# Padding tiles and a moved pool, so that the stage pools' tiles lie at multiples of 512 bytes

## The chip, the cores and the metric

The kernel runs on one core of a Trainium2 chip. TensorE multiplies, VectorE (DVE), ScalarE (ACT) and GpSimd (POOL) work on tiles, and SyncE (SP) issues nearly all DMAs. The metric is the time of the core in microseconds, as the median of several runs.

## The reference, cut to what matters

Two blocks run one after the other on 512 tokens of width 1024, in float32:

```python
# first block
h = rms_norm(x, ln_mix_g)
x = x + (sigmoid(m1) * (nsa_attention(h) @ w_branch_nsa) + sigmoid(m2) * (gla(h) @ w_branch_gla)) @ w_out
x = x + memory_cross_attention(rms_norm(x, ln_x_g), rms_norm(mem, ln_mem_g))   # @ w_xq, w_xkv, w_xo
x = x + ((gelu(conv3(u)) * g) @ w_down)        # u, g = split(rms_norm(x, ln_ffn_g) @ w_up), 2816 wide each
x = rms_norm(x, ln_final_g)
# second block
x = x + retention(rms_norm(x, ret_norm))       # 4 heads, w_in 1024x6144, w_out 2048x1024
x = x + ((silu(conv3(gate)) * val) @ w_down0)  # FFN, 2816 wide
x = x + stick_breaking(rms_norm(x, sb_norm))   # 16 heads of 64
x = x + ((silu(conv3(gate)) * val) @ w_down1)
return rms_norm(x, final_norm)
```

## The kernel before

**Products.** The activations are kept transposed, as 8 tiles xT of 128 x 512 floats. Every float32 operand of a large product is split into a rounded part (fp32r) and a rest, as hi and lo: `split` (L147) does it with one instruction of ScalarE (L148) and one of VectorE (L149). `mm3` (L171) then issues three products for each pair: both hi (L175), stationary hi with streamed lo (L176), stationary lo with streamed hi (L177). Each product loads a stationary operand of 128 columns (512 bytes in a partition) and streams a moving operand, mostly of 512 columns (2048 bytes). In the trace a product is written out<-moving,stationary.

**Weights.** `wload` (L159) brings a unit of 128 x 1024 floats by DMA into one of 2 buffers wr and splits it into one of 3 buffers wh and wl. A unit serves 24 products of 512 columns. In most projections (`fm_unit`, L179) the weight tile is stationary and the activation streams; in `tm_block` (L188) it is the other way round.

**Stages.** The program goes through the stages gla, nsa, mrg, xat (cross attention), ffa (first FFN), ret (retention), ffb, stk (stick-breaking) and ffc. Streamed by the large products are: xh and xl (the scaled input of each stage, split), mid (the hidden tiles of the FFNs, L854 and L149), yh and yl (outputs of retention heads), os (attention outputs), mix (the merged branches), ons (outputs of nsa), mm (the normalised memory, in mrg, both as moving and as stationary operand), wd (the weights of the last four outputs of ffc, as stationary operand, with 256 columns of mid), v and sT (values and scores of retention), pT (transposed weights of the nsa attention). The softmax of nsa reads a table, strip, that one DMA brings at the stage's start (L618).

**Places.** All tiles live in pools. The pools const, x, w and sm stand from low addresses up for the whole program; each `stage` opens two pools above them, first wk (all tiles of 2048 bytes) and then st, and closes them at its end; the pools mix and mem stand between sm and a stage's; the pool mixo (ons and share) stands at the other end. Tiles get addresses in the order of their pool. The pool sm holds small tiles and ends at 448 modulo 512. A tile's phase is its address in a partition modulo 512 bytes; the built programs have these:

| tiles | phase before | phase after |
|---|---|---|
| x, xh, xl (pool x); wr, wh, wl (pool w) | 0 | 0 |
| wk, mid, yh, yl, os, mix, mm, v, sT, kq, wd, khi, klo, qs, vhl, qh, ql, k, vh, hi, lo (stage pools, mix, mem) | 448 | 0 |
| ons, share (pool mixo) | 480 | 0 |
| pT of nsa | 288 | 0 |
| pr of nsa (transposed by TensorE) | 32 to 416 | 96 to 480 |
| pcmp and vcmp (pool sm) | 0 | 64 |
| rB, and acc of the sums of squares (pool sm) | 384, 0 | 448, 64 |
| sbtri_r, negones_r, negones (pool const, stationary in stk) | 448 | 448 |

The order of each engine's instructions is set by a scheduler when the program is built.

Of the kernel before, what the change touches and what calls it, by code (L numbers as in the profile page):

```python
# [10 lines left out]
F32 = mybir.dt.float32  # L11
F32R = mybir.dt.float32r
# [5 lines left out]
P = 128  # L18
# [47 lines left out]
def tile_blocks(ctx: ExitStack, tc: tile.TileContext, a: dict, out: bass.AP, dbg=None):  # L66
    nc = tc.nc
    act, dve, pool, pe, sync = nc.scalar, nc.vector, nc.gpsimd, nc.tensor, nc.sync

    cur = {}  # L70

    def sbpool(name, stack=ctx, side=None):
        kw = {} if side is None else {"side": side}
        return stack.enter_context(tc.tile_pool(name=name, bufs=1, reuse_waits="tile", **kw))
# [21 lines left out]
    def wkt(dt=F32):  # L96
        return cur["wk"].tile([P, S], dt, tag="wk", name="wk", bufs=cur["nwk"])

    def bank(tag="pa"):
        return cur["psum"].tile([P, S], F32, tag=tag, name=tag, bufs=cur["banks"][tag])  # L100
# [4 lines left out]
    def tiles(pool_, tag, n, bufs=None, dt=F32, w=S):  # L105
        return [pool_.tile([P, w], dt, tag=tag, name=tag, bufs=bufs or n) for _ in range(n)]
# [4 lines left out]
    sm_ = sbpool("sm")  # L111

    class sm:
        @staticmethod
        def tile(shape, dt, tag=None, name=None, bufs=4):
            return sm_.tile(shape, dt, tag=tag or name, name=name, bufs=bufs)


    g0 = cpool.tile([P, 2 * KD], F32, name="g0")
# [3 lines left out]
    def x_tile(k, dt=F32):  # L123
        return xpool.tile([P, S], dt, tag=f"x{k}", name=f"x{k}", bufs=1)
# [10 lines left out]
    def C(name, i=0, n=None):  # L135
        o, c = CST[name]
        return cst[:, o + i:o + i + (c if n is None else n)]
# [9 lines left out]
    def split(hi, lo, src):  # L147
        act.activation(hi, src, AF.Copy)  # L148
        dve.tensor_sub(lo, src, hi.bitcast(F32))  # L149
# [9 lines left out]
    def wload(src, own=None):  # L159
        n = src.shape[-1]  # L160
        raw = wpool.tile([P, UNIT], F32, tag="r", name="wr", bufs=NRAW)
        if own is None:
            hi = wpool.tile([P, UNIT], F32R, tag="h", name="wh", bufs=NSPL)
            lo = wpool.tile([P, UNIT], F32R, tag="l", name="wl", bufs=NSPL)
        else:
            hi, lo = own
        sync.dma_start(raw[:, :n], src)
        split(hi[:, :n], lo[:, :n], raw[:, :n])
        return hi, lo
# [143 lines left out]
    def mixer():  # L313
# [3 lines left out]
        with stage("gla", {"pp": 4, "pa": 3, "ss": 1}, 5) as st:  # L317
# [271 lines left out]
            for hd in range(4):  # L589
# [8 lines left out]
                hi, lo = x_tile(hd, F32R), x_tile(4 + hd, F32R)  # L598
# [7 lines left out]
        op = sbpool("mixo", hold, "right")  # L606
# [4 lines left out]
        def half_gate(m, j, dst):  # L611

            proj(16 + 8 * j + m, dst)
            act.activation(dst, dst, AF.Tanh, scale=0.5)

        with stage("nsa", {"pp": 2, "s": 3, "pt": 2, "po": 1}, 2) as st:
            strip = st.tile([P, NSTRIP], F32, name="strip")
            sync.dma_start(strip, a["strip"])  # L618

            pcmp = [sm.tile([P, S], F32R, tag="nrm", name="pcmp", bufs=3) for _ in range(2)]  # L620
            for x in pcmp:
                pool.memset(x.bitcast(F32), 0.0)

            def geometry(i):
                nk = P * (i + 1)
                w0 = P * max(0, i - 2)
                return nk, w0, nk - w0

            def softmaxes(kv, i):
                nk, w0, nw = geometry(i)  # L630
                nkp, nwp = max(256, nk), max(256, nw)
                ss = sm.tile([P, 4, 3], F32, tag="ss", name="ss")
                prs = []
                for g in range(4):
                    hd = 4 * kv + g
                    slope = 2.0 ** -(hd + 1)
                    qs = qh[hd][:, i * P:(i + 1) * P]
                    s0, s1 = bank("s"), bank("s")
                    for dst, (his, los), c in ((s0[:, :nkp], ks, slice(0, nkp)), (s1[:, :nwp], kw, slice(w0, w0 + nwp))):
                        pe.matmul(dst, qs, his[kv][:, c], start=True, stop=False)  # L640
                        pe.matmul(dst, qs, los[kv][:, c], start=False, stop=True)
                    for j in range(2):
                        pe.matmul(s1[:, 384:416], qs, kcmp[j][:, kv, :], start=j == 0, stop=j == 1)
                    pr = st.tile([P, NPR], F32, tag="pr", name="pr", bufs=5)
                    nm = sm.tile([P, 3], F32, tag="nm", name="nm")
                    c0 = 896 + 24 - 8 * i
                    segs = ((pr[:, 896:NPR], s1[:, 384:384 + NCMP], strip[:, c0:c0 + NCMP]),
                            (pr[:, 0:nk], s0[:, :nk], strip[:, 512 - nk:512]),
                            (pr[:, 512:512 + nw], s1[:, :nw], strip[:, 512 + 384 - nw:896]))
                    for b in (1, 2, 0):  # L650
                        dst, src, dist = segs[b]
                        dve.tensor_tensor_reduce(out=dst, in0=src, in1=dist, scale=slope, scalar=3e38, op0=OP.add,
                                                 op1=OP.min, accum_out=nm[:, b:b + 1])
                        act.activation(dst, dst, AF.Exp, scale=-1.0, bias=nm[:, b:b + 1],  # L654
                                       accum_out=ss[:, g, b:b + 1])
                    prs.append([x[0] for x in segs])
                dve.reciprocal(ss, ss)
                dve.tensor_mul(ss, ss, gates[:, i, 12 * kv:12 * kv + 12].rearrange("p (g b) -> p g b", g=4))
                if i == 0:
                    dve.tensor_mul(ss[:, :, 0], ss[:, :, 0], C("rowmask").to_broadcast([P, 4]))  # L660
                for g in range(4):
                    for b in (1, 2, 0):
                        scaler(b).tensor_scalar(prs[g][b], prs[g][b], ss[:, g, b:b + 1], 1.0, op0=OP.mult, op1=OP.mult)  # L663
                return prs

            def scaler(b):
                return pool if b == 1 else dve

            def values(kv, i, prs):
                nk, w0, nw = geometry(i)  # L670
                blocks = [(1, j * P, P, vhl[j][:, kv, :]) for j in range(i + 1)]
                blocks += [(2, j * P, P, vhl[w0 // P + j][:, 2 + kv, :]) for j in range(nw // P)]
                blocks += [(0, 0, NCMP, vcmp[:, kv, :])]
                po = bank("po")
                for x, (b, o, n, v) in enumerate(blocks):
                    pt = bank("pt")
                    for g in range(4):
                        pe.transpose(pt[0:n, g * P:(g + 1) * P], prs[g][b][:, o:o + n], ident)  # L678
                    hi, lo = tiles(st, "pT", 2, 4, F32R) if b else pcmp
                    split(hi[0:n], lo[0:n], pt[0:n])  # L680
                    for j, m in enumerate((hi, lo)):
                        pe.matmul(po, v, m, start=x + j == 0, stop=x == len(blocks) - 1 and j == 1)  # L682

                rows = slice(kv * 64, kv * 64 + 64)
                other = slice(64 - kv * 64, P - kv * 64)
                t = wkt()
                act.activation(t[rows], po[other], AF.Copy)
                dve.tensor_add(t[rows], t[rows], po[rows])
                src = t[rows].rearrange("p (g q) -> p g q", g=4)
                split(ons[0][rows, :, i * P:(i + 1) * P], ons[1][rows, :, i * P:(i + 1) * P], src)  # L690

            todo = [(kv, i) for kv in range(2) for i in (3, 2, 1, 0)]
            prev = None
            for kv, i in todo:
                prs = softmaxes(kv, i)
                if prev is not None:
                    values(*prev)
                prev = (kv, i, prs)
            values(*prev)
            ons_ = [(ons[0][:, g, :], ons[1][:, g, :]) for g in range(4)]  # L700


            share = tiles(op, "share", KD)
            for m2 in range(KD // 2):
                for m in (2 * m2, 2 * m2 + 1):
                    half_gate(m, 1, share[m])
                u = wload(a["w_branch_gla"][m2])
                for j in range(2):
                    m = 2 * m2 + j
                    pg = fm_unit(u, ogs, 4, off=j * 512)  # L710
                    dve.scalar_tensor_tensor(share[m], share[m], 1.0, pg, op0=OP.add, op1=OP.mult)
# [639 lines left out]
```

## Time and profile before

| | |
|---|---|
| median of 3 runs | 2341.67 us (2338.39 to 2344.12) |
| profiled execution | 2338.12 us, its span 2336.3 us |
| TensorE busy | 2294.6 us, 98% of the span, 10872 products |
| VectorE, ScalarE, GpSimd busy | 60%, 44%, 8% |
| mean granted clock of TensorE | 0.994 |

A product's record has a modelled end and is longer than the time to the next product's start; records overlap. Where TensorE has no idle time, the time goes by from start to start.

### The profile page before, as it was taken

How to read it: one execution, taken by the hardware profiler on the slowest of the kernel's cores; microseconds unless marked ns; L12 is line 12 of the kernel's file. 1: busy time of each engine (PE TensorE's matmuls, PEld its weight loads, DVE VectorE, ACT ScalarE, POOL GpSimd, SP SyncE). 2: the span in 40 equal slices, each digit the busy share in tenths (PEclk: the TensorE clock that was granted, in tenths of full speed). 3: DMA queues.
4: the chain of work that ended last, by engine and by line, in shares of the span. 5: the costliest groups of instructions: out<-in, count | busy, mean ns of one | idle time of the engine just before them, and what ended most of it. 6: DMA issues, size and time to landing. Idle time of an engine off the chain costs nothing.

```text
span 2336.3 us, 28002 instructions
## 1 busy us (share of the span) xinstructions
PE 2294.6 (98%) x10872; PEld 1881.3 (81%) x10872; DVE 1398.4 (60%) x2194; ACT 1021.6 (44%) x1662; POOL 194.0 (8%) x228
## 2 busy tenths in 40 slices
PE   8999999999999999999999999999999999999997
PEld 7787778878888888888887788888888887888886
DVE  5457875457545356545454674746577886747465
ACT  4345763444323234423323442424477884424243
POOL 2001110101000003000000100000121101000002
PEclk9999999999999999999999999999999999999998
DMA  4221032312222223222222232222344322222222
GB/s 159 91 64 54 28 118 98 115 66 100 99 91 99 95 90 113 82 91 81 81 90 73 81 108 90 99 92 93 98 118 105 91 64 81 99 98 92 99 92 71
DMA packets 66054, 213.41 MB, mean 91 GB/s; under 512 B 7793, under 2 KB 10114, under 8 KB 65794
## 3 DMA queue, kind: packets, MB, share of 16 engines
q1 hardware_dynamic: 60802, 203.24, 26.2%
q0 software_dynamic: 5120, 8.39, 1.7%
q8 instruction: 85, 1.39, 0.2%
q14 instruction: 47, 0.39, 0.1%
HBM read 201.11 MB, written 2.10 MB: 87 GB/s over the span
## 4 chain that ended last, share of the span: by engine, by line
PE 91%; DVE 4%; ACT 2%; issue 1%; POOL 1%; DMA 0%; SPq 0%; DVEq 0%; POOLq 0%; ACTq 0%
PE pp L176 26%; PE pp L175 26%; PE pp L177 26%; PE po L682 1%; DVE wl L149 1%; DVE xl L268 1%; PE pt L678 1%; ACT pr L654 1%; PE po L1143 1%; PE pp L1050 1%; PE pp L1052 1%; PE pp L1051 1%; POOL pr L663 1%; DVE x L298 1%; PE pa L982 1%
## 5 line engine op out<-in xcount | busy, mean ns | idle before, releaser
L148 ACT ACTIVATE wh<-wr 128x1024 fp32r<-128x1024 f32 (+2 forms) x368 | 384.3, 1044 | 790.4 <-PE pp L176 623.2
L175 PE MATMUL pp<-xh,wh 128*128 128x512 f32 x1612 | 634.9, 394 | 3.0 <-ACT xh L267 2.8
L176 PE MATMUL pp<-xl,wh 128*128 128x512 f32 x1612 | 631.8, 392 | 3.6 <-DVE xl L268 3.6
L177 PE MATMUL pp<-xh,wl 128*128 128x512 f32 x1612 | 632.0, 392 | 0.0
L149 DVE TENSOR_TENSOR wl<-wr,wh 128x1024 fp32r<-128x1024 f32 (+2 forms) x368 | 452.4, 1229 | 209.3 <-ACT wh L148 182.8
L175 PEld LDWEIGHTS pp<-xh,wh 128*128 128x128 f32 x1612 | 303.8, 189 | 66.8 <-ACT xh L267 4.1
L176 PEld LDWEIGHTS pp<-xl,wh 128*128 128x128 f32 x1612 | 303.9, 189 | 66.3 <-DVE xl L268 5.5
L177 PEld LDWEIGHTS pp<-xh,wl 128*128 128x128 f32 x1612 | 303.7, 188 | 62.7 <-issue 0.9
L298 DVE TENSOR_TENSOR x<-x,pp 128x512 f32<-128x512 f32 x130 | 89.2, 686 | 244.4 <-PE pp L177 244.3
L175 PE MATMUL pp<-mid,wh 128*128 128x512 f32 x504 | 198.9, 396 | 0.0
L176 PE MATMUL pp<-mid,wh 128*128 128x512 f32 x504 | 198.6, 395 | 0.0
L177 PE MATMUL pp<-mid,wl 128*128 128x512 f32 x504 | 198.5, 395 | 0.0
L237 POOL TENSOR_TENSOR acc<-acc 128x512 f32<-128x512 f32 (+1 forms) x60 | 80.4, 1340 | 913.0 <-ACT acc L233 839.1
L176 PE MATMUL pp<-wl,xh 128*128 128x512 f32 (+1 forms) x320 | 122.3, 382 | 4.0 <-DVE wl L149 4.0
L175 PE MATMUL pp<-wh,xh 128*128 128x512 f32 (+1 forms) x320 | 121.4, 381 | 0.8 <-ACT wh L148 0.8
L177 PE MATMUL pp<-wh,xl 128*128 128x512 f32 (+1 forms) x320 | 121.3, 380 | 0.0
L175 PEld LDWEIGHTS pp<-mid,wh 128*128 128x128 f32 x504 | 94.4, 187 | 24.8 <-ACT mid L148 2.0
L176 PEld LDWEIGHTS pp<-mid,wh 128*128 128x128 f32 x504 | 94.4, 187 | 23.7 <-DVE mid L149 0.9
L177 PEld LDWEIGHTS pp<-mid,wl 128*128 128x128 f32 x504 | 94.4, 187 | 22.8
L148 ACT ACTIVATE mid<-wk 128x512 fp32r<-128x512 f32 x66 | 41.5, 631 | 124.4 <-DVE wk L854 108.8
L827 ACT ACTIVATE wk<-wk,vec 128x512 f32<-128x512 f32 x110 | 88.6, 809 | 6.5 <-DVE wk L841 5.2
L829 DVE SCALAR_TENSOR_TENSOR wk<-wk,vec 128x510 f32<-128x510 f32 x110 | 82.3, 750 | 3.6
(426 smaller groups left out, 3369.3 us busy)
## 6 DMA issues: line engine op xcount, KB each, us to landing
wr<-in_up SPq DMA_DIRECT2D x88, 512.0 KB, 3.2
wr<-in_w_up SPq DMA_DIRECT2D x44, 512.0 KB, 3.2
wr<-in_w_in_fm SPq DMA_DIRECT2D x32, 512.0 KB, 3.6
wr<-in_ret_vg SPq DMA_DIRECT2D x32, 512.0 KB, 3.2
wr<-in_down SPq DMA_DIRECT2D x32, 512.0 KB, 3.2
wr<-in_w_down SPq DMA_DIRECT2D x16, 512.0 KB, 3.2
wr<-in_ret_qk SPq DMA_DIRECT2D x16, 512.0 KB, 3.3
wr<-in_ret_out SPq DMA_DIRECT2D x16, 512.0 KB, 3.3
```

The lines of the kernel that those rows point to most:

```text
L148: act.activation(hi, src, AF.Copy)
L149: dve.tensor_sub(lo, src, hi.bitcast(F32))
L175: pe.matmul(ps, sh, mh, start=first and i == 0, stop=False)
L176: pe.matmul(ps, sh, ml, start=False, stop=False)
L177: pe.matmul(ps, sl, mh, start=False, stop=last and i == n - 1)
L237: (dve if k == len(tiles) - 1 else pool).tensor_add(acc[:, :n], acc[:, :n], sq[:, :n])
L268: dve.scalar_tensor_tensor(lo, x, g, hi.bitcast(F32), op0=OP.mult, op1=OP.subtract)
L298: dve.tensor_add(xT[m], xT[m], ps)
L654: act.activation(dst, dst, AF.Exp, scale=-1.0, bias=nm[:, b:b + 1], accum_out=ss[:, g, b:b + 1])
L663: scaler(b).tensor_scalar(prs[g][b], prs[g][b], ss[:, g, b:b + 1], 1.0, op0=OP.mult, op1=OP.mult)
L827: act.activation(dst, src, AF.Identity, scale=V(wname, 2 * nw + j), bias=V(bname, j))
L829: dve.scalar_tensor_tensor(dst[:, 2:], src[:, :S - 2], V(wname, j), dst[:, 2:], op0=OP.mult, op1=OP.add)
```

## The change

A helper `fill` allocates a tile of n floats in a pool and sets it to zero. One of 16 floats (64 bytes) stands first in the pool sm, so that this pool, and all that stands above it, begins its tiles 64 bytes higher. One of 120 floats (480 bytes) stands last in mixo. The tiles pT of nsa go from the pool st, where they stood behind strip and pr, to the pool wk. The table above has the phases that follow.

```diff
@@ -114,6 +114,12 @@
         @staticmethod
         def tile(shape, dt, tag=None, name=None, bufs=4):
             return sm_.tile(shape, dt, tag=tag or name, name=name, bufs=bufs)
+
+    def fill(pool_, n):
+
+        pool.memset(pool_.tile([P, n], F32, name="fill"), 0.0)
+
+    fill(sm_, 16)
 
 
     g0 = cpool.tile([P, 2 * KD], F32, name="g0")
@@ -676,7 +682,7 @@
                     pt = bank("pt")
                     for g in range(4):
                         pe.transpose(pt[0:n, g * P:(g + 1) * P], prs[g][b][:, o:o + n], ident)
-                    hi, lo = tiles(st, "pT", 2, 4, F32R) if b else pcmp
+                    hi, lo = tiles(cur["wk"], "pT", 2, 4, F32R) if b else pcmp
                     split(hi[0:n], lo[0:n], pt[0:n])
                     for j, m in enumerate((hi, lo)):
                         pe.matmul(po, v, m, start=x + j == 0, stop=x == len(blocks) - 1 and j == 1)
@@ -701,6 +707,7 @@
 
 
             share = tiles(op, "share", KD)
+            fill(op, 120)
             for m2 in range(KD // 2):
                 for m in (2 * m2, 2 * m2 + 1):
                     half_gate(m, 1, share[m])
```

The instructions of TensorE, VectorE, ScalarE and SyncE stand in the same order in both programs; their lines are 6 or 7 higher after. GpSimd has two more, the memsets. Its rows at the start of the nsa stage, where it scales the softmax rows pr, with the semaphores that each waits for; before:

```order
L210 TENSOR_TENSOR y<-v,mhalf 128x16 [waits DVE_49]
L663 TENSOR_SCALAR pr<-pr,ss 128x512 [waits PE_49,DVE_49,Activation_49,Pool_49]
L663 TENSOR_SCALAR pr<-pr,ss 128x512 [waits Activation_49] x2
L663 TENSOR_SCALAR pr<-pr,ss 128x512 [waits DMAHW0_49,Activation_49]
L663 TENSOR_SCALAR pr<-pr,ss 128x384 [waits DVE_49,Activation_49]
```

and after:

```order
L216 TENSOR_TENSOR y<-v,mhalf 128x16 [waits DVE_49]
L120 MEMSET fill 128x120
L669 TENSOR_SCALAR pr<-pr,ss 128x512 [waits DVE_49,PE_49,Activation_49]
L669 TENSOR_SCALAR pr<-pr,ss 128x512 [waits PE_49,Activation_49,Pool_49]
L669 TENSOR_SCALAR pr<-pr,ss 128x512 [waits Activation_49] x2
L669 TENSOR_SCALAR pr<-pr,ss 128x384 [waits DVE_49,Activation_49]
```

The memset of 120 columns stands between two instructions of GpSimd and waits for nothing. On SyncE, at the same place of the program, the DMA of strip stands among loads of weights; before:

```order
L167 DMA wr<-in_w_in_fm 128x1024 [waits DMAHW7_49,DVE_49]
L167 DMA wr<-in_w_in_fm 128x1024 [waits DMAHW0_49,DVE_49]
L618 DMA strip<-in_strip 128x951 [waits DVE_49,PE_49,Pool_49]
L167 DMA wr<-in_w_branch_gla 128x1024 [waits DMAHW1_49,DVE_49]
L167 DMA wr<-in_w_in_fm 128x1024 [waits DMAHW2_49,DVE_49,Activation_49]
```

and after:

```order
L173 DMA wr<-in_w_in_fm 128x1024 [waits DMAHW7_49,DVE_49]
L173 DMA wr<-in_w_in_fm 128x1024 [waits DMAHW0_49,DVE_49]
L624 DMA strip<-in_strip 128x951 [waits Pool_49]
L173 DMA wr<-in_w_branch_gla 128x1024 [waits DMAHW1_49,DVE_49]
L173 DMA wr<-in_w_in_fm 128x1024 [waits DMAHW2_49,DVE_49,Activation_49]
```

Its place in the queue is the same, and it waits for one GpSimd instruction where it waited for VectorE, TensorE and GpSimd, since strip now lies over other tiles of the stage before.

## Rows read from the trace of the kernel before

**Rows 1.** Page, parts 1 and 4: TensorE's share; the chain by engine.

```profile
PE 2294.6 (98%) x10872; PEld 1881.3 (81%) x10872; DVE 1398.4 (60%) x2194; ACT 1021.6 (44%) x1662; POOL 194.0 (8%) x228
...
PE 91%; DVE 4%; ACT 2%; issue 1%; POOL 1%; DMA 0%; SPq 0%; DVEq 0%; POOLq 0%; ACTq 0%
```

**Rows 2.** Waits of TensorE, longest entry: us in total, times, longest.

```profile
PE pt L678 <- POOL pr L663: 4.0, 11, 0.7
```

**Rows 3.** TensorE by shape: count, busy us, mean ns, idle us before.

```profile
L175 PE MATMUL pp<-xh,wh 128*128 128x512 f32 x1612 | 634.9, 394 | 3.0 <-ACT xh L267 2.8 <-ACT wh L148 0.2
...
L175 PE MATMUL pp<-mid,wh 128*128 128x512 f32 x504 | 198.9, 396 | 0.0
...
L175 PE MATMUL pp<-wh,xh 128*128 128x512 f32 x288 | 112.4, 390 | 0.0
...
L175 PE MATMUL pp<-yh,wh 128*128 128x512 f32 x96 | 38.1, 397 | 0.0
...
L175 PE MATMUL pp<-os,wh 128*128 128x512 f32 x76 | 30.8, 406 | 0.3 <-DVE x L298 0.3
...
L175 PE MATMUL pp<-mix,wh 128*128 128x512 f32 x64 | 25.3, 395 | 0.0
...
L175 PE MATMUL pp<-ons,wh 128*128 128x512 f32 x32 | 12.7, 396 | 0.0
```

**Rows 4.** Two stretches of ffa by tile: ns min/median/max, first and last start.

```profile
L175 PE MATMUL pp<-mid,wh x64: 394/394/394, 625.5 to 669.6; 128*128 128x512 f32 x64
...
L175 PE MATMUL pp<-xh,wh x128: 388/389/395, 670.3 to 756.7; 128*128 128x512 f32 x128
```

**Rows 5.** Timeline, ends of stretches in ffa and ffc: start and duration, us.

```profile
625.50 0.39 PE L175 MATMUL pp<-mid,wh 128*128 128x512 f32 x1
...
670.06 0.39 PE L177 MATMUL pp<-mid,wl 128*128 128x512 f32 x1
670.29 0.39 PE L175 MATMUL pp<-xh,wh 128*128 128x512 f32 x1
...
757.13 0.39 PE L177 MATMUL pp<-xh,wl 128*128 128x512 f32 x1
...
2042.15 0.39 PE L175 MATMUL pp<-mid,wh 128*128 128x512 f32 x1
...
2086.90 0.39 PE L177 MATMUL pp<-mid,wl 128*128 128x512 f32 x1
```

**Rows 6.** By tile, whole span: four other pairs of phases.

```profile
L176 PE MATMUL po<-v,sT x40: 387/389/395, 974.0 to 1261.0; 128*128 128x512 f32 x40
...
L175 PE MATMUL pp<-wh,mm x16: 396/397/398, 448.0 to 458.5; 128*128 128x512 f32 x16
...
L175 PE MATMUL pp<-mm,wh x32: 276/276/283, 459.2 to 469.8; 128*128 128x256 f32 x32
...
L176 PE MATMUL pp<-mid,wd x48: 274/283/283, 2301.6 to 2319.4; 128*128 128x256 f32 x48
```

**Rows 7.** Timeline, ends of two stretches at 256 columns.

```profile
459.24 0.28 PE L175 MATMUL pp<-mm,wh 128*128 128x256 f32 x1
...
470.03 0.28 PE L177 MATMUL pp<-mm,wl 128*128 128x256 f32 x1
...
2307.84 0.28 PE L177 MATMUL pp<-mid,wd 128*128 128x256 f32 x1
...
2309.28 0.28 PE L177 MATMUL pp<-mid,wd 128*128 128x256 f32 x1
```

**Rows 8.** A memset of GpSimd by shape; the wait of strip's DMA.

```profile
L1031 POOL MEMSET negones<- 128x128 f32 x1 | 0.2, 196 | 0.0
...
SPq L618 <- PE s L641: 1.7, 1, 1.7
```

**Rows 9.** Windows: busy us (instructions) of each engine, granted clock, DMA, GB/s.

```profile
105.00:115.40 10.40, 10.40 (x86) 9.20 (x86) 3.20 (x8) 2.72 (x7) 0.00 (x0) 1.00 0.16 52
115.50:125.70 10.20, 10.20 (x47) 7.89 (x47) 3.28 (x8) 4.75 (x8) 0.00 (x0) 0.50 0.00 0
```

## The prediction

> **What bounds the kernel now.** I read the page first. TensorE is busy in 98% of the span and 91% of the chain that ended last is TensorE's [rows 1]. Then the waits of TensorE: the longest entry is 4.0 us in 11 waits [rows 2]. The table of its shapes shows where that time is spent: products with 128 rows and 512 columns, of xh and xl, of mid, of yh, of os, of mix and of ons, with next to no idle time before them [rows 3]. So the kernel is a queue of products with nobody else late, and its time is the number of products times the step from one to the next. The question is whether the step depends on where the operands lie.
>
> A record's own duration (389 or 394 ns) is longer than the step, because products overlap. I therefore take the step from starts. In the first FFN, 192 products of mid (three lines of 64 [rows 4]) start from 625.50 to 670.06 us [rows 5]: 44.56 us for 191 steps, 233.3 ns. The 384 products of xh and xl that follow (128 of each of three lines [rows 4]) start from 670.29 to 757.13 us [rows 5]: 86.84 us for 383 steps, 226.7 ns. Both stretches run at the full clock without a wait, both multiply with wh and wl, and both have a weight load to each product. In the third FFN the 192 products of mid take 2042.15 to 2086.90 us [rows 5], 234.3 ns. So one kind of product is 6.6 to 7.6 ns dearer than the other.
>
> What differs is the place. By the address table above, xh and xl lie at phase 0 (bytes modulo 512) and mid at phase 448, while wh and wl are at 0. Three explanations fit these two stretches alone: a streamed operand off 512 is slow; tiles of the stage's pool are slow; or a streamed operand whose phase is not that of the stationary operand loaded meanwhile is slow. Other groups decide [rows 6]. v and sT both lie at 448, in the stage's pool, and take 389 ns as xh does: the first two explanations fall. wh at 0 streamed past the stationary mm at 448 takes 397 ns, with a step of (458.5 - 448.0) us / 45 = 233.3 ns, though wh streamed past xh takes 390 ns [rows 3]. So it is the difference of phases. At 256 columns the sign is the other way: mm (448) against wh (0) takes 276 ns, mid (448) against wd (448) 283 ns; in steps, (470.03 - 459.24) us / 95 = 113.6 ns (3 x 32 products) and (2309.28 - 2307.84) us / 12 = 120.0 ns (13 rows in succession) [rows 7].
>
> **The change part by part.** It moves tiles and no instruction of TensorE, VectorE, ScalarE or the DMA queue changes its place; two memsets on GpSimd are added.
>
> Stage pools from 448 to 0. mid has 3 x 504 = 1512 products at 512 columns [rows 3]: each FFN multiplies 22 tiles of mid into 8 outputs with three lines, 528 products, but the third runs the last 6 tiles in this shape for only 4 of the 8 outputs, 456. Their phase becomes that of wh and wl. First FFN: 528 x 6.6 ns = 3.5 us. The second and third FFN at the third's price: 984 x 7.6 ns = 7.5 us. Together 11.0 us.
>
> The other products that go from unequal to equal: yh and yl 288, os 240 (76 x 3, and by the code 12 into bank zA), mix 192, ons 96 (phase 480 to 0 by the second fill), wh against mm 48. Their records take the long form (394 to 397 ns [rows 3, 6]), so 864 x 6.6 ns = 5.7 us. Some of os, in the stick-breaking stage, stand between attention products; I count them in full, since no wait of that stage is among the long ones [rows 2].
>
> What becomes dearer: mm against wh at 256 columns goes from unequal to equal, 96 x (120.0 - 113.6) ns = 0.6 us. Three constant tiles (sbtri_r, negones_r, negones) stay at 448 while the tiles streamed against them go to 0; about 160 products of 256 to 512 columns become unequal, gaining at 256 what they lose at 512. I take nothing, with 0.3 us either way.
>
> pT in the nsa stage (76 x 2 products, phase 288 to 0 by its move to the other pool): half of them are followed by a transpose or a wait, and each could gain at most 6.6 ns, under 1.0 us. I take nothing.
>
> The two fills are memsets of 16 and of 120 columns; the nearest row, 128 columns, is 0.2 us [rows 8]. The first stands at the start, ahead of four other memsets, while the first inputs are still on their way; the second stands where GpSimd waits for its first scaling. The strip's DMA no longer waits for the last products of the stage before: the queue lost 1.7 us there [rows 8], and what is behind it (weights loaded ahead) had room. Bounds: 0.3 us lost to 1.7 us gained; I take nothing, since TensorE has products of xh in that place.
>
> What hides the rest: each unit of weights serves 24 products, 5.4 us at the fast step, and the products of xh already draw units at that pace without waiting [rows 3]. Nothing else comes due.
>
> **Sum:** 11.0 + 5.7 - 0.6 = 16.1 us. The profiled execution took 2338.12 us (span 2336.3 us, 1.8 us around it) and becomes 2322.0 us. The median of the runs is 3.55 us above it; taking the same off it, 2341.67 - 16.1 = 2325.6 us.
>
> Bounds: the records differ by 394 - 389 = 5 ns; if only that goes, 2376 x 5 ns - 0.6 us = 11.3 us, 2330.4 us. If every one of them is worth the dearest step, 2376 x 7.6 ns - 0.6 us = 17.5 us, and with the strip's 1.7 us and pT's 1.0 us 20.2 us: 2321.5 us. The runs before lie 2.5 to 3.3 us around their median.
>
> **A rule against it.** The same streamed wh takes 397 ns past mm [rows 6] and 390 ns past xh [rows 3]. The Trainium skill's page "TensorE: Matmul & The Clock Gate", under "Step-by-step: what each phase is for", says that the streamed operand and the weight load have two independent read ports and that loading the next weights takes no read bandwidth from the running matmul. By that rule no address matters and the sum would be zero; the trace disagrees by 5 to 8 ns a product.
>
> **The rivals.**
> *The ports are independent and the steps differ for another reason* (what is streamed was written lately, or its stage is busier). Then nothing moves: 2341.7 us. For it: the prices of mid differ between stages (233.3 and 234.3 ns) at one address phase. Against it: v and sT, and wh against mm [rows 6]. Chance 0.05.
>
> *The clock takes it back.* From 115.5 to 125.7 us the granted clock is 0.50, the 1.2 GHz level, after 10.4 us of 86 small products at 1.00 [rows 9]. A stretch like this costs at most half of its 10.2 us, 5.1 us. Two more of them leave 16.1 - 10.2 = 5.9 us: 2335.8 us, no change that can be told. For it: such stretches stand in the attention stages, whose tiles and waits shift a little. Against it: TensorE's order is untouched. Chance 0.06.
>
> *Equal phases are the dear ones.* At 256 columns they are, by 6.4 ns. If a stage tile against a weight tile (a pair never seen at equal phase here, since v and sT lie in one pool) behaved so at 512 columns, 2376 x 6.4 ns = 15.2 us would be added: 2356.9 us, slower. It decides where the new step of mid is over 233.3 ns. Against it: xh against wh, equal and 226.7 ns, at many distances between the two. Chance 0.03.
>
> **How the numbers follow.** The forecast has 0.86. Measurement tells about 0.3% (7 us) from no change, so faster means below 2334.6 us: nearly all of the forecast, and a little of the clock's case, 0.88. Within 0.3%: the ports and most of the clock, 0.09. Slower: 0.03. The range takes both bounds with the scatter of a median, some 2 to 3 us: 2319.5 to 2333.5 us.
>
> **What would show it.** In the profile after, the stretch of 192 mid products in the first FFN should span 43.3 us instead of 44.56, with records of 389 ns; yh, os, mix and ons should show 389 too; mm against wh should go from 276 to 283 ns; xh and xl should stay at 226.7 ns. If mid stays at 394 ns, the phase was not the cause. If all this comes and the time does not, the loss stands as new idle time of TensorE, in the attention stages or at a stage's start.

## The result, and the profile after

The changed kernel takes 2328.21 us (median of 6 runs, 2324.86 to 2331.12), the kernel before in runs beside it 2342.01 us (2338.39 to 2344.12). The ratio is 0.9944, 95% interval 0.9930 to 0.9958: faster by 9.8 to 16.4 us. The prediction was 2325.6 us, 2.6 us too low, inside its range. The profiled execution took 2327.03 us, its span is 2325.3 us, 11.0 us less than before.

Page of the changed kernel, parts 1 and 4 (the three lines of `mm3` are now L181, L182 and L183):

```profile
PE 2283.8 (98%) x10872; PEld 1885.1 (81%) x10872; DVE 1397.9 (60%) x2194; ACT 1021.8 (44%) x1662; POOL 193.5 (8%) x230
...
PE 91%; DVE 4%; ACT 2%; issue 1%; POOL 1%; DMA 0%; SPq 0%; DVEq 0%; POOLq 0%; ACTq 0%
```

TensorE's busy time fell by 10.8 us, with the same 10872 products; that of VectorE, ScalarE and GpSimd moved by less than 1 us [rows 1]. So the gain is in the products themselves. TensorE by shape (count, busy us, mean ns, idle us before):

```profile
L181 PE MATMUL pp<-xh,wh 128*128 128x512 f32 x1612 | 634.5, 394 | 3.4 <-ACT xh L273 3.2 <-ACT wh L154 0.2
L181 PE MATMUL pp<-mid,wh 128*128 128x512 f32 x504 | 196.6, 390 | 0.3
...
L181 PE MATMUL pp<-yh,wh 128*128 128x512 f32 x96 | 37.5, 391 | 0.0
L181 PE MATMUL pp<-os,wh 128*128 128x512 f32 x76 | 30.6, 402 | 0.3 <-DVE x L304 0.3
L181 PE MATMUL pp<-mix,wh 128*128 128x512 f32 x64 | 25.0, 391 | 0.0
```

xh keeps its 394 ns; mid went from 396 to 390, yh from 397 to 391, mix from 395 to 391, os from 406 to 402 [rows 3]. A few longer records are in these means; by tile, the median record of each of them, and of ons, is 389 ns. The two FFN stretches of ffa in the timeline, ends of the 192 mid products and of the 384 products of xh and xl (start us, duration us):

```profile
626.42 0.39 PE L181 MATMUL pp<-mid,wh 128*128 128x512 f32 x1
...
669.71 0.39 PE L183 MATMUL pp<-mid,wl 128*128 128x512 f32 x1
669.94 0.39 PE L181 MATMUL pp<-xh,wh 128*128 128x512 f32 x1
...
756.75 0.39 PE L183 MATMUL pp<-xh,wl 128*128 128x512 f32 x1
```

43.29 us for 191 steps is 226.7 ns, where it was 233.3 [rows 5]; xh's 86.81 us for 383 steps is 226.7 ns, as it was. In what follows I give the price of **a triple** (the three products of `mm3`) in a long stretch: here 43.29 / 191 x 3 = 680.0 ns, before 44.56 / 191 x 3 = 699.9 ns.

The other pairs, tile by tile (ns min/median/max, first and last start):

```profile
L181 PE MATMUL pp<-wh,mm x16: 389/389/389, 447.2 to 457.4; 128*128 128x512 f32 x16
...
L181 PE MATMUL pp<-mm,wh x32: 277/283/283, 458.1 to 469.3; 128*128 128x256 f32 x32
```

wh past mm went from 397 to 389 ns, and mm past wh at 256 columns from 276 to 283: at 512 columns equal phases are cheaper and at 256 dearer, as read from [rows 6].

**Where the gain fell short.** In ffc the 192 mid products take this (timeline of TensorE, ScalarE and VectorE; in brackets the idle time before and its end):

```profile
2033.39 0.39 PE L181 MATMUL pp<-mid,wh 128*128 128x512 f32 x1
...
2037.89 0.63 ACT L154 ACTIVATE mid<-wk 128x512 fp32r<-128x512 f32 x1 [2.75 <-DVE wk L861]
...
2037.92 0.39 PE L183 MATMUL pp<-mid,wl 128*128 128x512 f32 x1
2038.15 0.92 PE L181 MATMUL pp<-mid,wh 128*128 128x512 f32 x2
...
2038.55 0.69 DVE L155 TENSOR_TENSOR mid<-wk,mid 128x512 fp32r<-128x512 f32 x1 [0.70 <-ACT mid L154]
...
2038.91 0.40 PE L182 MATMUL pp<-mid,wh 128*128 128x512 f32 x1
...
2077.03 0.39 PE L183 MATMUL pp<-mid,wl 128*128 128x512 f32 x1
```

and before, the same place:

```profile
2046.82 0.39 PE L177 MATMUL pp<-mid,wl 128*128 128x512 f32 x1
2047.05 0.79 PE L175 MATMUL pp<-mid,wh 128*128 128x512 f32 x2
...
2047.68 0.39 PE L176 MATMUL pp<-mid,wh 128*128 128x512 f32 x1
```

Three steps, from the L183 product to the L182 product, take 2038.91 - 2037.92 = 0.99 us after, where 3 x 0.227 = 0.68 are due: 0.31 us of waiting. Before they took 2047.68 - 2046.82 = 0.86 us, where 3 x 0.233 = 0.70 are due: 0.16 us. The second product of the pair at 2038.15 multiplies the last tile of mid, whose hi part ScalarE finishes at 2037.89 + 0.63 = 2038.52 us. TensorE waited for it before too. Now it gets there earlier, since its 20 steps so far are shorter, and waits longer. Of the 191 steps the others are at the fast pace: (43.64 - 0.31) us / 191 = 226.9 ns.

**The clock.** Two new stretches of 3.3 us at half the clock are in this execution (busy us and count of PE, PEld, DVE, ACT, POOL; granted clock, DMA share, GB/s):

```profile
20.90:24.20 3.30, 3.30 (x14) 3.30 (x15) 1.60 (x2) 0.00 (x0) 0.53 (x1) 0.50 0.72 212
543.20:546.50 3.30, 3.30 (x9) 2.60 (x8) 1.63 (x4) 0.00 (x0) 0.38 (x1) 0.50 0.09 14
```

In the profile before both windows were granted 1.00, with 22 and 16 products. The long stretch of [rows 9] stands as it was, 1 us later.

### The profile page after: what moved, and what is told of

The parts are those of the page before. It is cut to its first block, busy times and chain, and to the rows that moved or that the text cites. A ratio compares the mean times of both kernels' runs of the same rounds, so it can differ in the third digit from the quotient of the medians.

```text
span 2325.3 us, 28003 instructions
## 1 busy us (share of the span) xinstructions
PE 2283.8 (98%) x10872; PEld 1885.1 (81%) x10872; DVE 1397.9 (60%) x2194; ACT 1021.8 (44%) x1662; POOL 193.5 (8%) x230
## 4 chain that ended last, share of the span: by engine, by line
PE 91%; DVE 4%; ACT 2%; issue 1%; POOL 1%; DMA 0%; SPq 0%; DVEq 0%; POOLq 0%; ACTq 0%
PE pp L182 26%; PE pp L181 26%; PE pp L183 26%; DVE wl L155 1%; PE po L688 1%; DVE xl L274 1%; PE pt L684 1%; PE po L1150 1%; PE pp L1057 1%; PE pp L1058 1%; PE pp L1059 1%; POOL pr L669 1%; DVE x L304 1%; ACT pr L660 1%; PE pa L989 1%
## 5 line engine op out<-in xcount | busy, mean ns | idle before, releaser
L181 PE MATMUL pp<-xh,wh 128*128 128x512 f32 x1612 | 634.5, 394 | 3.4 <-ACT xh L273 3.2
L182 PE MATMUL pp<-xl,wh 128*128 128x512 f32 x1612 | 631.9, 392 | 3.6 <-DVE xl L274 3.6
L183 PE MATMUL pp<-xh,wl 128*128 128x512 f32 x1612 | 632.2, 392 | 0.0
L181 PEld LDWEIGHTS pp<-xh,wh 128*128 128x128 f32 x1612 | 303.9, 189 | 66.8 <-ACT xh L273 4.4
L182 PEld LDWEIGHTS pp<-xl,wh 128*128 128x128 f32 x1612 | 303.8, 188 | 66.2 <-DVE xl L274 5.7
L183 PEld LDWEIGHTS pp<-xh,wl 128*128 128x128 f32 x1612 | 303.9, 189 | 62.6 <-issue 0.9
L181 PE MATMUL pp<-mid,wh 128*128 128x512 f32 x504 | 196.6, 390 | 0.3
L182 PE MATMUL pp<-mid,wh 128*128 128x512 f32 x504 | 196.0, 390 | 0.0
L183 PE MATMUL pp<-mid,wl 128*128 128x512 f32 x504 | 195.8, 389 | 0.0
L182 PE MATMUL pp<-wl,xh 128*128 128x512 f32 (+1 forms) x320 | 123.2, 385 | 3.5 <-DVE wl L155 3.5
L181 PE MATMUL pp<-wh,xh 128*128 128x512 f32 (+1 forms) x320 | 122.4, 385 | 0.3 <-ACT wh L154 0.3
L183 PE MATMUL pp<-wh,xl 128*128 128x512 f32 (+1 forms) x320 | 122.2, 383 | 0.0
L181 PEld LDWEIGHTS pp<-mid,wh 128*128 128x128 f32 x504 | 94.6, 188 | 22.2 <-ACT mid L154 2.8
L182 PEld LDWEIGHTS pp<-mid,wh 128*128 128x128 f32 x504 | 94.6, 188 | 20.4 <-DVE mid L155 1.1
L183 PEld LDWEIGHTS pp<-mid,wl 128*128 128x128 f32 x504 | 94.6, 188 | 19.5
```

The source lines that it names most:

```text
L181: pe.matmul(ps, sh, mh, start=first and i == 0, stop=False)
L182: pe.matmul(ps, sh, ml, start=False, stop=False)
L183: pe.matmul(ps, sl, mh, start=False, stop=last and i == n - 1)
```

## The experiments

All of them start from the changed kernel, and their edits are given against it. The run of before beside each set took 2340.13 us (the first four), 2339.62 us (the next four), 2339.36 us (wl alone, paired outputs) and 2341.47 us (xl alone, wh alone). Where an edit adds lines, the three lines of `mm3` stand up to 5 lower in the profile.

### All pools at phase 448

```diff
     pool.memset(mhalf, -0.5)
+    fill(cpool, 112)
...
-            fill(op, 120)
+            fill(op, 8)
```

Is it the multiple of 512, or that the phases are the same?

> Every tile of the x, w, stage and mixo pools lies at phase 448, none at a multiple of 512. Theory (equal phases of streamed and loaded operand are fast at 512 columns): steps of xh, xl and mid stay at 226.7 ns with records of 389 ns, and the time is that of the changed kernel, 2328 us within its scatter of 3 us. Rival (an operand must itself lie at a multiple of 512): some 8300 products at 512 columns take 233.3 ns, 39 us more than before, about 2381 us.

2328.06 us, ratio 0.9951 (0.9936 to 0.9966). Tiles in ffa:

```profile
L181 PE MATMUL pp<-mid,wh x64: 389/389/389, 626.3 to 669.2; 128*128 128x512 f32 x64
```

No streamed or loaded tile of these products lies at a multiple of 512 any more, and mid still has the fast form. So the multiples of 512 in the change's name do nothing; that streamed and stationary tiles have the same phase does.

### Weights and stage at 448, xh and xl at 0

```diff
+    fill(wpool, 112)
     fill(sm_, 16)
...
-            fill(op, 120)
+            fill(op, 8)
```

This keeps mid equal to the weights and takes xh away from them.

> The weight tiles wr, wh, wl and the stage pools lie at phase 448; xh and xl stay at 0. Theory: mid against wh is equal and stays at 226.7 ns, xh against wh becomes unequal and goes to 233.3 ns, some 5900 products x 6.6 ns = 39 us, less 384 products of 256 columns x 6.4 ns = 2.5 us that become faster; 2328 + 36.5 = 2364.5 us. Rival (the streamed operand must lie at a multiple of 512): xh stays at 226.7 ns and mid goes back to 233.3 ns, about 2342 us.

2343.21 us, ratio 1.0016 (1.0005 to 1.0027). Tiles of mid in ffa:

```profile
L182 PE MATMUL pp<-mid,wh x64: 389/389/395, 635.6 to 678.5; 128*128 128x512 f32 x64
```

Timeline, ends of the 384 products of xh and xl in ffa:

```profile
679.14 0.40 PE L182 MATMUL pp<-xh,wh 128*128 128x512 f32 x1
...
766.82 0.39 PE L184 MATMUL pp<-xh,wl 128*128 128x512 f32 x1
```

The time alone would fit the rival's 2342 us, but the steps do not: mid stayed at 226.8 ns, 448 against 448, and xh at a multiple of 512 became dearer. So the rival falls, and with it that something else than the phase made the kernel faster. But the size was wrong: 87.68 us / 383 x 3 = 686.8 ns for a triple, 6.8 ns above equal phases and not 20. Where wh (448) is streamed past xh (0) the step is 233.3 ns, the full price. In these stretches the same two tiles have two prices, by which of them is streamed: streamed 64 above the stationary one (modulo 256 or 512) 6.8 ns a triple, streamed 64 below it 20. It is not so everywhere: 48 products of xh and xl in xat, at the same addresses, take the full 233.4 ns (47 steps from 550.45 to 561.42 us).

### Stage pools at 256

```diff
-    fill(sm_, 16)
+    fill(sm_, 80)
...
-            fill(op, 120)
+            fill(op, 56)
```

> The stage pools and mixo lie at phase 256, the weights at 0. If the phase counts modulo 512: mid at 233 ns, mm against wh back at 113.6 ns, about 2342 us as before. If it counts modulo 256 or less: mid at 226.7 ns, 2328 us.

2326.75 us, ratio 0.9942 (0.9926 to 0.9959). Tiles in ffa:

```profile
L181 PE MATMUL pp<-mid,wh x64: 389/389/390, 625.5 to 668.4; 128*128 128x512 f32 x64
```

256 against 0 is equal: phases count modulo 256 bytes (or a part of it; 128 comes below). So 448 stands 64 below the weights' 0, or 192 above.

### The first fill alone

```diff
-                    hi, lo = tiles(cur["wk"], "pT", 2, 4, F32R) if b else pcmp
+                    hi, lo = tiles(st, "pT", 2, 4, F32R) if b else pcmp
...
-            fill(op, 120)
```

> Only the first fill: the second one and the move of pT are taken back, so ons lies at 480 and pT at 352, the rest as in the changed kernel. Theory: mid, mix, yh, os at 226.7 ns as in the changed kernel; ons back at 233 to 235 ns, 96 x 7 ns = 0.7 us; pT under 1 us; 2328 to 2330 us. Rival (the gain comes from the freer start of the strip's DMA and of the nsa stage): back to 2342 us with mid at 226.7 ns.

2328.30 us, ratio 0.9952 (0.9938 to 0.9967). Tiles of ons:

```profile
L181 PE MATMUL pp<-ons,wh x32: 395/396/397, 348.7 to 403.1; 128*128 128x512 f32 x32
```

ons has its old price, by the steps 96 x 6.6 ns = 0.6 us, too little to be told in the total. One padding tile of 64 bytes in a partition does the work; pT's move and the second fill are worth nothing that a median shows.

### Stage pools at 64, 128 and 32

```diff
-    fill(sm_, 16)
+    fill(sm_, 32)
...
-            fill(op, 120)
+            fill(op, 104)
```

The other two are fills of 48 and 88 floats (phase 128), and of 24 and 112 (phase 32).

> The stage pools and mixo lie at phase 64, the weights at 0: mid streamed 64 bytes past the phase of wh, where before it was 64 bytes short of it. If only the size of the difference counts: mid at 233.3 ns, 2341 us. If its sign counts (e2 had xh 64 bytes past wh at 228.9 ns): mid at 228.9 ns and wh against mm at 233 ns, 2328 + 2376 x 2.2 ns = 2333 us.

> The stage pools and mixo lie at phase 128, the weights at 0. If phases count modulo 256, mid is unequal: 233 ns (or 229 ns, if the sign counts), 2333 to 2341 us. If they count modulo 128: mid at 226.7 ns, 2327 us as with 256.

> The stage pools and mixo lie at phase 32, the weights at 0. If any difference modulo 256 is dear alike: mid at 233 ns, 2341 us. If the price grows with the difference: mid between 226.7 and 230 ns, under 2335 us.

At 64: 2332.86 us, ratio 0.9973 (0.9961 to 0.9985). At 128: 2338.65 us, 0.9993 (0.9983 to 1.0002). At 32: 2341.81 us, 1.0008 (0.9999 to 1.0018). The ends of the 192 mid products in ffa, first with the stage at 64:

```profile
628.64 0.40 PE L181 MATMUL pp<-mid,wh 128*128 128x512 f32 x1
...
672.38 0.39 PE L183 MATMUL pp<-mid,wl 128*128 128x512 f32 x1
```

at 128:

```profile
625.55 0.40 PE L181 MATMUL pp<-mid,wh 128*128 128x512 f32 x1
...
670.12 0.39 PE L183 MATMUL pp<-mid,wl 128*128 128x512 f32 x1
```

and at 32:

```profile
631.38 0.40 PE L181 MATMUL pp<-mid,wh 128*128 128x512 f32 x1
...
675.95 0.40 PE L183 MATMUL pp<-mid,wl 128*128 128x512 f32 x1
```

A triple is 43.74 / 191 x 3 = 687.0 ns at 64, and 44.57 / 191 x 3 = 700.1 ns at 128 and at 32. So it is not modulo 128, the price doesn't grow with the distance, and the sign counts: mid streamed 64 above the weights pays a third of what it paid 64 below them (448) before. Why it is so no run shows. With the stage at 64 the reverse pair, wh streamed past mm, lies 64 below and has the long record:

```profile
L181 PE MATMUL pp<-wh,mm x16: 394/394/394, 450.8 to 461.3; 128*128 128x512 f32 x16
```

With the stage at 128 the 96 products of mm past wh at 256 columns start so:

```profile
458.75 0.28 PE L181 MATMUL pp<-mm,wh 128*128 128x256 f32 x1
...
470.15 0.28 PE L183 MATMUL pp<-mm,wl 128*128 128x256 f32 x1
```

That is 11.40 us for 95 steps, 120.0 ns, the price of equal phases. So at 256 columns not every difference is cheap.

### wd taken off the stage's phase

```diff
         w = len(mid) * P
+        fill(st, 16)
         us = [wload(a[name][m], tiles(st, "wd", 2, 2 * NHALF, F32R, w)) for m in range(m0, KD)]
```

At 256 columns unequal phases were the cheap ones in [rows 7]. Can the 144 products of mid past wd gain?

> The changed kernel with 64 bytes of padding ahead of the wd tiles alone, so that 144 products of 256 columns (mid at 0 against wd at 64) become unequal. Theory (at 256 columns unequal is the fast form): steps from 120.0 to 113.6 ns, 0.9 us less, 2327 us, which the time cannot tell from 2328. Rival (the 113.6 ns of mm have another cause): 120.0 ns stays.

2327.85 us, ratio 0.9946 (0.9928 to 0.9964).

```profile
L181 PE MATMUL pp<-mid,wd x48: 276/281/367, 2287.6 to 2305.1; 128*128 128x256 f32 x48
```

The first 90 of these products stand in succession; their ends in the timeline:

```profile
2287.64 0.28 PE L181 MATMUL pp<-mid,wd 128*128 128x256 f32 x1
...
2298.12 0.28 PE L183 MATMUL pp<-mid,wd 128*128 128x256 f32 x1
```

The median record went from 283 to 281 ns. The step over the 90 is 10.48 us / 89 = 117.8 ns, where it is 119.9 in the changed kernel, and not the 113.6 of mm. The sign is as forecast, the size depends on the pair; 144 x 2.1 ns = 0.3 us can't be seen in the total.

### wl alone off, xl alone off, wh alone off

Which products pay when only one of the operands of a triple is off? Three kernels; in the last two the fill behind share is left out as well. wl at 64:

```diff
-    fill(sm_, 16)
+    gap = []
...
             hi = wpool.tile([P, UNIT], F32R, tag="h", name="wh", bufs=NSPL)
+            if not gap:
+                gap.append(fill(wpool, 16))
             lo = wpool.tile([P, UNIT], F32R, tag="l", name="wl", bufs=NSPL)
```

xl at 192, which is 64 below its neighbours modulo 256:

```diff
-    xhl = [[xpool.tile([P, KD // 2, S], F32R, name=f"x{c}{i}") for i in range(2)] for c in "hl"]
+    xhl = []
+    for c, n in ("h", 48), ("l", 16):
+        xhl.append([xpool.tile([P, KD // 2, S], F32R, name=f"x{c}{i}") for i in range(2)])
+        pool.memset(xpool.tile([P, n], F32, name=f"fill{c}"), 0.0)
```

wh at 64, wl at 256:

```diff
+    gap = []
...
+            if len(gap) == 0:
+                gap.append(fill(wpool, 16))
             hi = wpool.tile([P, UNIT], F32R, tag="h", name="wh", bufs=NSPL)
+            if len(gap) == 1:
+                gap.append(pool.memset(wpool.tile([P, 48], F32, name="fill2"), 0.0))
```

> The changed kernel with wl alone moved to phase 64; wh, xh, xl and mid stay at 0. Of the three products of a triple the third (stationary wl) is then the one whose own stationary operand is unequal, and the second is the one that streams while wl is loaded for the next. If the load under way counts: the second product goes from 226.7 to 233 ns and the first and third stay. If the product's own stationary operand counts: the third goes to 233 ns. Either way about 2400 triples x 6.6 ns = 16 us more, 2344 us.

> Only the tiles xl stand off: phase 192 (64 bytes below a multiple of 256); xh 0, weights and stage 256, which counts as 0 by the run with stage pools at 256. The fill behind share is left out, so ons stays off. In the run with wl alone at 64 the triple xh,wh / xl,wh / xh,wl took 693.5 ns instead of 680. If one weight load collides with two streams (the one before its own product and its own), the price belongs to the stream and is paid once here: triple 686.7 ns, 1936 triples x 6.6 ns = 12.8 us, with ons' 0.6 us 2341.6 us. If each change between unequal and equal is what costs, the triple has two changes again: 693.5 ns, 2354.5 us.

> Only the tiles wh stand off, at 64, and wl, xh, xl and the stage's tiles at 0 or 256; the fill behind share is left out. If one load collides with two streams, all three streams of a triple meet a load of wh: 680 + 3 x 6.6 = 700 ns, about 2690 triples x 20 ns = 53 us, some 2382 us. If a load collides with one stream only, or if each change costs, two of three are dear: 693.3 ns, 36 us, 2364 us.

wl: 2358.30 us, ratio 1.0077 (1.0060 to 1.0095), 14 us more than expected under either rule. xl: 2343.70 us, 1.0011 (1.0002 to 1.0021). wh: 2373.51 us, 1.0149 (1.0131 to 1.0167). The ends of the 384 products of xh and xl in ffa, with wl off:

```profile
676.09 0.39 PE L183 MATMUL pp<-xh,wh 128*128 128x512 f32 x1
...
764.60 0.40 PE L185 MATMUL pp<-xh,wl 128*128 128x512 f32 x1
```

with xl off:

```profile
674.50 0.39 PE L181 MATMUL pp<-xh,wh 128*128 128x512 f32 x1
...
762.17 0.39 PE L183 MATMUL pp<-xh,wl 128*128 128x512 f32 x1
```

and with wh off:

```profile
680.40 0.39 PE L186 MATMUL pp<-xh,wh 128*128 128x512 f32 x1
...
768.91 0.39 PE L188 MATMUL pp<-xh,wl 128*128 128x512 f32 x1
```

A triple is 88.51 / 383 x 3 = 693.3 ns with wl off, 87.67 / 383 x 3 = 686.7 ns with xl off and 88.51 / 383 x 3 = 693.3 ns with wh off: 13.3, 6.7 and 13.3 ns above equal phases.

None of the three rules explains all of it. "Each change between unequal and equal costs" wanted 13.3 for xl: it falls. "A load collides with two streams" fits wl and xl and wanted 20 for wh: it falls. "A load collides only with the stream under way" fits xl and wh and wanted 6.7 for wl: it falls too, as does the rule that only a product's own stationary operand counts, which wl alone had been to tell from it. In the program as a whole the wh kernel is 9.5 us dearer than the 2364 us of its nearest case, since in other stretches its triples cost more than in this one. The ends of the same 384 products of ffb:

```profile
1467.77 0.40 PE L186 MATMUL pp<-xh,wh 128*128 128x512 f32 x1
...
1557.13 0.40 PE L188 MATMUL pp<-xh,wl 128*128 128x512 f32 x1
```

There a triple takes 89.36 / 383 x 3 = 700.0 ns, with the tiles at the phases that they have in ffa. So the phases alone do not settle the price of an unequal pair, and a rule can't be told from one stretch. Which load meets which stream stays open.

### The first two outputs of ffb and ffc together

```diff
-    def out_proj(name, rhs):
+    def out_proj(name, rhs, pair=False):
+        if pair:
+            n = len(rhs)
+            us = [wload(a[name][m]) for m in range(2)]
+            pss = [proj_ps() for _ in us]
+            for ks in (range(n - 1), range(n - 1, n)):
+                for (hi, lo), ps in zip(us, pss):
+                    for k in ks:
+                        c = slice(k * P, (k + 1) * P)
+                        mm3(ps, [((hi[:, c], lo[:, c]), rhs[k])], first=k == 0, last=k == n - 1)
+            for m in range(2):
+                add_x(m, pss[m])
         for m in range(KD):
+            if pair and m < 2:
+                continue
...
-            out_proj(f"{down}_{part}", mid)
+            out_proj(f"{down}_{part}", mid, second is not None)
```

If the dearer step of ffb and ffc is only the wait for the last mid tile, then using that tile last, for two outputs at once, takes it away.

> The changed kernel, in the second and third FFN with the first two outputs of each down projection taken together: both are multiplied with all but the last mid tile, and then both with the last. Theory (the first output stands waiting for the last mid tile, 0.31 us at the start of each of these stretches, since the faster products reach it earlier): the two long steps of 423 and 338 ns are gone, 6 x 0.31 = 1.8 us less, 2326 us. Rival (the long steps belong to the start of a stretch, as a fetch or a bank does): they stay, 2328 us.

2325.47 us, ratio 0.9940 (0.9924 to 0.9955). Timeline of the same stretch of ffc:

```profile
2033.59 0.39 PE L181 MATMUL pp<-mid,wh 128*128 128x512 f32 x1
...
2037.89 0.39 PE L182 MATMUL pp<-mid,wh 128*128 128x512 f32 x1
2038.12 0.39 PE L183 MATMUL pp<-mid,wl 128*128 128x512 f32 x1
2038.35 0.39 PE L181 MATMUL pp<-mid,wh 128*128 128x512 f32 x1
2038.57 0.39 PE L182 MATMUL pp<-mid,wh 128*128 128x512 f32 x1
...
2076.88 0.39 PE L183 MATMUL pp<-mid,wl 128*128 128x512 f32 x1
```

The long steps are gone and the stretch takes 43.29 us, to 0.01 us that of ffa. So ffc's products cost what ffa's do, and the rest of its time was waiting: shown. The last 72 of ffc's products go through another function, were not paired and keep their two long steps (451 and 335 ns). The total, 2.7 us below the changed kernel's, can't be told from it by these runs (the intervals overlap).

## Why the prediction was right, point by point

**The cause.** That the step depends on the difference of phases between what is streamed and the stationary tiles held: moving the stage removes the price, moving all pools together leaves it removed, and moving the weights brings it back for xh. The closer wording, the stationary operand that is loaded meanwhile, is not borne out: for wl alone it calls for 6.7 ns a triple, and 13.3 were measured. And one price for all unequal pairs, 6.6 ns a product, held because each was read at the phases of the kernel before; with the stage 64 above the weights it is a third of that. The rule cited in the prediction (the Trainium skill, "TensorE: Matmul & The Clock Gate", section "Step-by-step: what each phase is for") had two read ports that don't disturb each other; these runs disagree with it by 6.7 to 20 ns in a triple. With it falls the rival of independent ports, and that of dear equal phases: mid's step fell to 226.7 ns.

**mid, 11.0 us forecast, 8.85 measured** (the steps of all its 512-column products, before less after). The step that failed is "the second and third FFN at the third's price": 7.6 ns taken from the ends of a stretch in ffc as if each step were dearer. Only two steps were, by 0.16 us in all, and the median step there was 233 ns in both FFNs. That is 984 x 1.0 ns = 1.0 us too much. And the waits grew, here from 0.16 to 0.31 us: the six such stretches give back 0.13 to 0.21 us each, 1.1 us, and the third of ffa has a wait of 0.1 us that it did not have. 11.0 - 1.0 - 1.1 - 0.1 = 8.8 us.

**The other products, 5.7 us forecast, 4.7 measured**: yh and yl 1.77, mix 1.13, os 0.81, ons 0.65, wh past mm 0.32. All near the forecast but os, counted in full at 240 x 6.6 = 1.6 us. In xat 0.46 of 0.63 us came; in the stick-breaking stage, where os stands between attention products, 0.35 of 0.95 us. That the rows of the waits showed no long wait of that stage was no ground for counting it in full.

**mm past wh, 0.6 us lost**: measured 0.61 us (113.5 to 119.9 ns over 96). The constants, pT and strip, taken at nothing, gave nothing that shows.

**The sum** of the measured steps is 8.85 + 4.68 - 0.61 = 12.9 us, against 16.1 forecast and 13.8 us between the medians (9.8 to 16.4). The profiled executions differ by 11.0 us only. The rest of 1.9 us is the clock's: the profile after has one more short stretch at 0.50 than the one before (two new ones, and one at 1951.8 us gone). Both programs issue the same products in the same order, so their starts can be compared one by one: the changed kernel loses 1.5 us across the first new stretch and 1.6 across the second, and gains 1.1 where the old one is gone, 2.0 us in all. Neither comes with the change every time: the kernel with all pools at 448, which has the same steps, was granted 1.00 through its first 40 us, and the one with wd moved had 1.00 from 530 to 560 us. So the clock's rival, two more long stretches, did not come.

**The range** held, with bounds built from a record's 5 ns and the 7.6 ns step. The fast end of it rested on the step that was read wrongly.

## What to carry to other kernels

Where one engine is busy all the time, compare the start-to-start step of stretches that should be alike; a few ns a product in ten thousand products is worth more than any wait left. Look at the median step as well as at the ends of a stretch: ends divided by a count turn one wait into a price per instruction, and a wait grows when the price falls. And before aligning anything, try which of the alignments counts: here it was that the operands agree modulo 256 bytes, and one padding tile of 64 bytes gave it.

## What the runs showed of the hardware

- For float32 products split into rounded parts, 128 rows, 128 stationary and 512 streamed columns, with a weight load to each, a triple took 680.0 ns when all operands agreed modulo 256 bytes.
- When they did not, a triple of ffa cost more by about 6.7, 13.3 or 20 ns: 6.8 and 7.0 (streamed 64 above the stationary tiles), 19.9 (64 below), 20.1 (32 or 128 above), 6.7 (xl alone off), 13.3 (wl alone or wh alone off). Other stretches have values between these: wh past xh with wl alone off 15.8 ns, yh with the stage at 128 17.4 ns.
- A mixed layout can cost more than a uniform one: wl alone off cost 15 us more in the program than weights and stage off together (2358.3 and 2343.2 us).
- At 256 columns equal phases took 119.9 ns a product. Unequal ones took 113.5 (mm at 448, wh at 0) and 117.8 (wd moved by 64), but 120.0 with mm 128 above wh.
- The phases do not settle the price of an unequal pair. In the kernel before, wh streamed past mm lies 64 above it and yet took the full 233.3 ns [rows 6], where mid 64 above the weights took 229.0; and with wh alone off the same products of xh and xl took 693.3 ns a triple in ffa and 700.0 in ffb. What else decides, and why the sign counts, stays open.
